# Step sizes first, second convolutions and GLU handed out between the SSD chunks

## The chip, the cores and the metric

The kernel runs on one core of a Trainium2 chip. The metric is the device time of one execution in microseconds; the median of three runs of the kernel before is 2591.2 us (2588.39 to 2594.27). TensorE (PE) multiplies, VectorE (DVE), ScalarE (ACT) and GpSimd (POOL) do the elementwise work, and SyncE (SP) starts most DMAs; ACT starts a few.

## The reference

One encoder layer for two sequences (256 and 1024 tokens, kept here as 1280 columns of one [1024, 1280] matrix), all in float32:

```
h = rmsnorm(x);  u, z, xbc, dt, gates = split(h @ w_in)
s5 = s5_mixer(u)            # bidirectional complex scan, gelu, then h * sigmoid(h @ w_glu + b)
s5 = s5 @ w_s5_out
xbc = silu(conv4(xbc));  dt = softplus(dt + bias)
y  = d_skip * xs + ssd(xs, dt, a, B, C) + reversed ssd      # chunks of 128 tokens
m2 = group_rmsnorm(y * silu(z)) @ w_m2_out
x  = x + (gate0 * s5 + gate1 * m2) @ w_o
x  = x + relu(rmsnorm(x) @ w_up)^2 @ w_down;   out = rmsnorm(x)
```

## The kernel before

Each large product is made of three float32r matmuls (`mm3`: low x high, high x low, high x high parts); `load_w` loads a weight block on SP, ACT makes its high part (L117) and POOL its low part (L118). A "tile" of the input projection is 128 output rows by 1280 tokens: 3 pieces of 512, 512 and 256 columns, 8 x 3 matmuls each, 72 in all, into the two PSUM banks called `mm`. The code is written in the order of the program; a list scheduler then fixes one order of instructions for every engine, by program order and by blocks marked urgent. Each engine follows its order strictly, so an instruction that waits holds back everything behind it, DMA issues on SP and on ACT included.

The stages, with the names that matter here:

- S5: `s5_setup`, `s5_run`, and beside it on PE the 16 gate tiles `G` (`gate_tile`).
- `conv_tile(j, q)`, the list `X(j)`: five projection tiles of group j, then convolution and silu on DVE and ACT in the buffers `xpad` (two) and `ac` (one), and stores to DRAM (`xbc_d`, `xz_d`). `z_tile(j, q)`, the list `Z(j)`: three tiles with silu. There are four groups j.
- `dt_proc`: one projection tile, then some 50 elementwise steps on DVE for dt, its running sums (`dte`, `dtf`) and their logarithms, stored as 24 rows to DRAM (`es_d`, `cs_d`, `ns_d`), and small matmuls (`dg`, `dtf`) for the chunk decays.
- 40 chunks (four groups of ten). `chunk_in` transposes a chunk (`xt`) and carries the backward state; `chunk_loads` loads `bc`, `ec`, `er`, `el`, `xz` for the present and next chunk; `chunk_out` makes the decay matrices (matmuls `ex`, exponential `e`), the matmuls `y`, the result `yt` and its sums of squares `ssg`; `norm_factors` makes the row factors of a group (`rows`, to `rs_d`). `er`, `el`, `eye` and `out_of` are constant tiles, filled once.
- Between chunks the list `left` hands out remaining `conv_tile` and `z_tile` calls, so many per chunk.
- GLU, for two halves of 640 tokens: six loads `y` from DRAM and their parts (`yx`), six gated tiles (`w_glu`, tanh `th`, `s5`, parts `sx`), eight output tiles (`w_s5`, DVE into `t1`, stored in `ma_d`). Each of the 14 tiles is 36 matmuls of 320 columns. They stand behind the chunks in program order; the scheduler lifts them into gaps.
- `normed`: for 432 tokens the factors `rg` (from `rs_d`) and twelve tiles `wt` (from `w_d`) become twelve pairs of parts `gx` (DVE, ACT, DVE). `merge` multiplies them by `w_m2` (36 matmuls per output tile, parts `mer`), `residual` by `w_o`; three times. Then the MLP, from about 1675 us to the end.

The lines that the prediction speaks of: dt on DVE L370 to L428; the stores of `parts` L408; the fills L550 to L557; the chunk matmuls L588 to L621; `yt` L624 to L627; the GLU L684 to L709; `normed` L655 to L662 with `hi_lo` L648 and L649; `hnw` L670.

Of the kernel before, what the change touches and what calls it, by code (L numbers as in the profile page):

```python
# [8 lines left out]
F32 = mybir.dt.float32  # L9
F32R = mybir.dt.float32r  # L10
# [45 lines left out]
def tile_encoder(ctx: ExitStack, tc: tile.TileContext, a: dict, dbg=None):  # L56
# [49 lines left out]
    def urgent():  # L106
        return tc.high_priority(offset=URG) if URG else ExitStack()
# [53 lines left out]
    with ExitStack() as pctx:  # L161
# [185 lines left out]
        def emit(l):  # L347
            for f, *r in l:
                f(*r)
        emit(G(0, 16) + X(0)[:2])  # L350
        kp = pctx.enter_context(tc.tile_pool(name="ssdk", bufs=1))
        dst, dec = (kp.tile([P, 10, 48], F32, name=n) for n in ("dst", "dec"))

        def dt_proc():

            with tc.tile_pool(name="dtp", bufs=1) as dp:
# [43 lines left out]
                def parts(src, dst_):  # L400
                    hl2 = [T(f"{src.name}p{i}", F32R) for i in range(2)]
                    act.activation(hl2[0], src, AF.Copy)
                    dve.tensor_tensor(hl2[1], src, hl2[0], SUB)
                    for i in range(2):
                        for h in range(2):
                            for d in range(2):
                                r = 64 * h + 32 * d
                                nc.sync.dma_start(dst_(i, d)[:, :, h * HT:h * HT + HT], hl2[i][r:r + 24].bitcast(F32))  # L408
# [4 lines left out]
                parts(e, lambda i, d: cs_d[:, d, i])  # L413
                dve.tensor_scalar(q, v, 1e-37, None, MAX)
                act.activation(q, q, AF.Ln)
                dve.tensor_tensor(q, q, e, SUB)
                parts(q, lambda i, d: ns_d[:, d, :, i])
                dve.tensor_tensor(f, f, n, SUB)
                act.activation(f, f, AF.Exp)
                dve.tensor_tensor(f, f, v, MUL)  # L420
# [117 lines left out]
            rsqrt(nc, r, ms, t)  # L538
            nc.sync.dma_start(rs_d[j, k0:k0 + n], r)

        NR = 2
        ers = [sp.tile([P, 6, P], F32R, name=f"er{i}", bufs=1) for i in range(NR)]
        els = [sp.tile([P, 2, P], F32R, name=f"el{i}", bufs=1) for i in range(NR)]
        for i in range(NR):
            B6 = [P, 6, P]
            pick = lambda o: ident[:, 4 + o:16 + o:2].unsqueeze(2).to_broadcast(B6)
            dve.tensor_tensor(ers[i], pick(0), pick(1), ADD)  # L550
            for d in range(2):
                dve.tensor_tensor(els[i][:, d], *(ident[:, c:c + 1].to_broadcast([P, P]) for c in (2 * d, 2 * d + 1)), ADD)

        eye = sp.tile([P, P], F32R, name="eye", bufs=1)
        dve.tensor_copy(eye, ident)
        out_of = sp.tile([P, 2, P], F32R, name="out_of", bufs=1)
        dve.tensor_scalar(out_of.rearrange("p i l -> p (i l)"), C("low", 0, 2 * P), BIG, BIG, MUL, SUB)  # L557
        nth = [0]

        def chunk_loads(j, k):  # L560
# [18 lines left out]
        def chunk_out(j, k, xt, sf, sb, ssum):  # L579
# [52 lines left out]
            dve.tensor_tensor(sq[:, 0], sq[:, 0], sq[:, 1], ADD)  # L632
            dve.tensor_tensor(ssum, sq[:, 0], sq[:, 2], ADD)

        ins = [(j, k) for j in range(4) for k in (1, 0, 9, 8, 7, 6, 5, 4, 3, 2)]
# [35 lines left out]
    with ExitStack() as gctx:  # L671
        gp = gctx.enter_context(tc.tile_pool(name="glu", bufs=1, side="right"))
        hb = gctx.enter_context(tc.tile_pool(name="glub", bufs=2, side="right"))
        hbg = gp.tile([P, 6], F32, name="hbg")
        dve.tensor_scalar(hbg, V("bglu", 0, 6), 0.5, None, MUL)
        for hf in range(2):
            t0 = hf * HT
            if hf:
                gx = normed(*cs[0])
            y0, yx, sx = [], [], []  # L680
            with urgent():
                for k in range(6):
                    r = gp.tile([P, HT], F32, name=f"y{k}")
                    nc.scalar.dma_start(r, y_d[k, hf].rearrange("p t n -> p (t n)"))  # L684
                    y0.append(r)
                    yx.append(split(gp, f"yx{k}", r, (pool, dve)[k % 2]))
            for m in range(6):
                w = load_tile(a["w_glu"][m])
                th = hb.tile([P, HT], F32, name="th5")
                s5 = hb.tile([P, 80, 8], F32, name="s5")  # L690
                for c0 in (0, 320):
                    pt = bank("mm")
                    mm3(pt[:, :320], w, yx, slice(c0, c0 + 320))
                    with urgent():
                        act.activation(th[:, c0:c0 + 320], pt[:, :320], AF.Tanh, scale=0.25, bias=hbg[:, m:m + 1])
                with urgent():
                    dve.scalar_tensor_tensor(s5.rearrange("p c t -> p t c"),
                                             th.rearrange("p (t c) -> p t c", t=8), 1.0,
                                             y0[m].rearrange("p (t c) -> p t c", t=8), ADD, MUL)
                    sx.append(split(gp, f"sx{m}", s5.rearrange("p c t -> p (c t)"), (pool, dve)[m % 2]))  # L700
            for m in range(8):
                w = load_tile(a["w_s5"][m])
                t1 = hb.tile([P, HT], F32, name="t1")
                nc.sync.dma_start(t1, gate_d[m, :, t0:t0 + HT])
                for c0 in (0, 320):
                    pt = bank("mm")
                    mm3(pt[:, :320], w, sx, slice(c0, c0 + 320))
                    dve.scalar_tensor_tensor(t1[:, c0:c0 + 320], t1[:, c0:c0 + 320], 1.0, pt[:, :320], ADD, MUL)
                nc.sync.dma_start(ma_d[m, :, t0:t0 + HT], t1)  # L709
# [624 lines left out]
```

## Time and profile before

| what | us |
|---|---|
| median of three runs | 2591.2 |
| the profiled execution | 2594.99 |
| its span, first to last instruction | 2593.2 |
| PE busy | 2490.3 |
| DVE busy | 1488.2 |
| ACT busy | 949.0 |
| POOL busy | 780.6 |

PE's busy time is the union of its matmuls, which overlap each other; a matmul's own duration is longer than the distance to the next. The granted clock is the share of full speed (2.4 GHz) that TensorE had; 0.5 is 1.2 GHz. A wait is put down to what ended it last.

### The profile page before, as it was taken

How to read it: one execution, taken by the hardware profiler on the slowest of the kernel's cores; microseconds unless marked ns; L12 is line 12 of the kernel's file. 1: busy time of each engine (PE TensorE's matmuls, PEld its weight loads, DVE VectorE, ACT ScalarE, POOL GpSimd, SP SyncE). 2: the span in 40 equal slices, each digit the busy share in tenths (PEclk: the TensorE clock that was granted, in tenths of full speed). 3: DMA queues.
4: the chain of work that ended last, by engine and by line, in shares of the span. 5: the costliest groups of instructions: out<-in, count | busy, mean ns of one | idle time of the engine just before them, and what ended most of it. 6: DMA issues, size and time to landing. Idle time of an engine off the chain costs nothing.

```text
span 2593.2 us, 37087 instructions
## 1 busy us (share of the span) xinstructions
PE 2490.3 (96%) x14119; PEld 2135.8 (82%) x14119; DVE 1488.2 (57%) x2445; ACT 949.0 (37%) x1867; POOL 780.6 (30%) x558
## 2 busy tenths in 40 slices
PE   8999999979999999988989999999999999999998
PEld 6788888868888888877879899988888888888887
DVE  7899999782457667678652654433333333323336
ACT  7655554343445445454332434311111111111114
POOL 2511112111111111134244757632222222222235
PEclk9999999989999999999999999999999999999999
DMA  4323333233345545465556766431111111111113
GB/s 148 105 84 99 96 96 94 91 121 106 132 138 168 156 134 164 144 188 153 180 160 190 223 188 206 151 122 37 37 37 41 37 37 37 41 37 37 37 45 114
DMA packets 254434, 286.21 MB, mean 110 GB/s; under 512 B 29864, under 2 KB 186704, under 8 KB 254256
## 3 DMA queue, kind: packets, MB, share of 16 engines
q1 hardware_dynamic: 252528, 279.90, 34.5%
q10 hardware_dynamic: 1728, 3.93, 0.5%
q8 instruction: 112, 1.84, 0.3%
q14 instruction: 66, 0.54, 0.1%
HBM read 210.26 MB, written 73.50 MB: 109 GB/s over the span
## 4 chain that ended last, share of the span: by engine, by line
PE 69%; DVE 17%; DMA 6%; ACT 3%; issue 2%; POOL 1%; SPq 1%; DVEq 0%; ACTq 0%; POOLq 0%
PE pa L142 24%; PE mm L133 20%; PE pa L133 9%; PE mm L142 8%; DVE z L1179 1%; PE ps L475 1%; PE y L621 1%; DVE z L1178 1%; DMA wt<-w_d 1%; DMA raw<-w_m 1%; PE ex L608 1%; PE ba L597 1%; PE ex L610 1%; DVE gx L649 1%; DVE wt L662 1%
## 5 line engine op out<-in xcount | busy, mean ns | idle before, releaser
L118 POOL TENSOR_TENSOR wl<-raw,wh 128x512 fp32r<-128x512 f32 (+1 forms) x422 | 582.0, 1384 | 1683.9 <-ACT wh L117 1600.9
L117 ACT ACTIVATE wh<-raw 128x512 fp32r<-128x512 f32 (+1 forms) x422 | 258.8, 615 | 922.8 <-PE pa L142 522.8
L133 PE MATMUL mm<-hh,wl 128*128 128x512 f32 (+1 forms) x1272 | 465.1, 366 | 14.9 <-ACT hh L220 7.5
L133 PE MATMUL mm<-hl,wh 128*128 128x512 f32 (+1 forms) x1272 | 465.9, 366 | 0.0
L133 PE MATMUL mm<-hh,wh 128*128 128x512 f32 (+1 forms) x1272 | 465.7, 366 | 0.0
L133 PEld LDWEIGHTS mm<-hh,wl 128*128 128x128 f32 x1272 | 242.5, 191 | 56.2 <-POOL wl L118 6.7
L133 PEld LDWEIGHTS mm<-hl,wh 128*128 128x128 f32 x1272 | 242.3, 190 | 41.5 <-issue 3.2
L133 PEld LDWEIGHTS mm<-hh,wh 128*128 128x128 f32 x1272 | 242.5, 191 | 40.9 <-issue 4.1
L142 PE MATMUL pa<-hid,wh 128*128 128x512 f32 (+1 forms) x1008 | 254.6, 357 | 0.0
L802 DVE TENSOR_TENSOR acc<-acc,pa 128x512 f32<-128x512 f32 (+1 forms) x252 | 138.2, 595 | 140.4 <-PE pa L142 140.4
L142 PEld LDWEIGHTS pa<-hid,wh 128*128 128x128 f32 x1008 | 170.3, 188 | 29.8
L786 DVE SCALAR_TENSOR_TENSOR r<-pa,rs 128x512 f32<-128x512 f32 (+1 forms) x72 | 39.6, 596 | 230.0 <-PE pa L142 230.0
L133 PE MATMUL pa<-gx,wh 128*128 128x432 f32 (+1 forms) x576 | 158.5, 356 | 0.0
L142 PE MATMUL pa<-xnh,wl 128*128 128x512 f32 (+1 forms) x576 | 155.9, 357 | 0.0
L142 PE MATMUL pa<-xnl,wh 128*128 128x512 f32 (+1 forms) x576 | 155.0, 357 | 0.0
L142 PE MATMUL pa<-xnh,wh 128*128 128x512 f32 (+1 forms) x576 | 154.0, 357 | 0.0
L142 PE MATMUL pa<-hid,wl 128*128 128x512 f32 (+1 forms) x504 | 143.4, 356 | 0.0
L318 DVE SCALAR_TENSOR_TENSOR ac<-xpad,hcw,ac 128x1282 f32<-128x1282 f32 x60 | 93.9, 1565 | 44.8 <-ACT ac L316 44.4
L142 PEld LDWEIGHTS pa<-xnh,wh 128*128 128x128 f32 x576 | 96.5, 188 | 17.9
L133 PEld LDWEIGHTS pa<-gx,wh 128*128 128x128 f32 x576 | 108.3, 188 | 3.6
L142 PEld LDWEIGHTS pa<-xnh,wl 128*128 128x128 f32 x576 | 96.5, 188 | 17.8
L142 PEld LDWEIGHTS pa<-xnl,wh 128*128 128x128 f32 x576 | 96.4, 188 | 17.9
(457 smaller groups left out, 4865.5 us busy)
## 6 DMA issues: line engine op xcount, KB each, us to landing
raw<-w_in SPq DMA_DIRECT2D x110, 256.0 KB
raw<-w_m SPq DMA_DIRECT2D x72, 256.0 KB
raw<-w_dn SPq DMA_DIRECT2D x72, 256.0 KB
raw<-w_up SPq DMA_DIRECT2D x64, 256.0 KB
ec<-es_d SPq DMA_DIRECT2D x80, 192.0 KB
xz<-xz_d SPq DMA_DIRECT2D x40, 384.0 KB
raw<-w_o SPq DMA_DIRECT2D x48, 256.0 KB
gate_d<-gv SPq DMA_DIRECT2D x16, 640.0 KB
```

What stands on the lines that cost most here:

```text
L117: act.activation(wh[:, :n], raw[:, :n], AF.Copy)
L118: pool.tensor_tensor(wl[:, :n], raw[:, :n], wh[:, :n], SUB)
L133: pe.matmul(out, l, r[:, sl], start=(n == 0), stop=(n == last))
L142: pe.matmul(o, l, r[:, sl], start=(n == 0), stop=(n == last))
L318: dve.scalar_tensor_tensor(ac[:, :n], xp[:, k:k + n], w(k), ac[:, :n], MUL, ADD)
L475: pe.matmul(st[:, :384], xt[:, 384:512], xs, start=True, stop=True)
L597: pe.matmul(bk[:, q * P:(q + 1) * P], st[:, q * P:(q + 1) * P], cf, start=True, stop=True)
L608: pe.matmul(ps[:, d].rearrange("p (h l) -> p h l", h=3), eye, out_of[:, d:d + 1].to_broadcast([P, 3, P]), start=True, stop=False)
L610: pe.matmul(ps[:, d], el[:, d], er[:, 3 * hh_:3 * hh_ + 3].rearrange("p h l -> p (h l)"), start=False, stop=True)
L621: pe.matmul(y[e0 * 64:e0 * 64 + 64, q * P:(q + 1) * P], xt[:, h * 64:h * 64 + 64], G[h // 3][:, h % 3], start=True, stop=True)
L786: dve.scalar_tensor_tensor(r[:, s], pt, 0.0, rs2[:, s], MAX, MUL)
L802: dve.tensor_tensor(ac[:, m, s], ac[:, m, s], pt, ADD)
```

## The change

Four moves, no arithmetic changed:

1. `dt_proc` comes right after the gate tiles, ahead of all convolution tiles (it stood behind the first two). The constant tiles `er`, `el`, `eye`, `out_of` are filled ahead of it, in a pool of their own, not in the memory that dt's temporaries leave. The stores of the second `parts` call (`ns_d`) are issued on ACT, not on SP.
2. Only `X(0)` and `Z(0)` come before the chunks; `X(1)` (five tiles) joins the list `left`, now 24 tiles.
3. `left` is handed out as two tiles after each of the first two chunks, one after the third, then 0.8 per chunk (0.7 before).
4. When `left` is empty (after the 27th chunk) the GLU memory is opened, and two of 30 GLU steps (per half: one load, six gated tiles, eight output tiles) follow each chunk. What is left of them comes after the last chunk, behind the first `normed`.

```diff
-        emit(G(0, 16) + X(0)[:2])
+        emit(G(0, 16))
         kp = pctx.enter_context(tc.tile_pool(name="ssdk", bufs=1))
+        ers = [kp.tile([P, 6, P], F32R, name=f"er{i}", bufs=1) for i in range(NR)]
...
-                parts(q, lambda i, d: ns_d[:, d, :, i])
+                parts(q, lambda i, d: ns_d[:, d, :, i], nc.scalar)
...
         dt_proc()
-        emit(X(0)[2:] + Z(0) + X(1))
-        left = Z(1) + X(2) + Z(2) + X(3) + Z(3)
+        emit(X(0) + Z(0))
+        left = X(1) + Z(1) + X(2) + Z(2) + X(3) + Z(3)
...
-        ers = [sp.tile([P, 6, P], F32R, name=f"er{i}", bufs=1) for i in range(NR)]
...
+        gctx, glu = ExitStack(), []
+        def glu_open():
+            rctx.close()
+            gp = gctx.enter_context(tc.tile_pool(name="glu", bufs=1, side="right"))
...
+            for hf in range(2):
+                glu.append(lambda hf=hf: load(hf))
+                for m in range(6):
+                    glu.append(lambda m=m: gated(m))
+                for m in range(8):
+                    glu.append(lambda m=m, hf=hf: s5_out(m, hf * HT))
...
                 chunk(j, k)
-                while left and 10 * (n_left - len(left)) < 7 * (10 * j + k + 1):
+                i = 10 * j + k + 1
+                while left and 10 * (n_left - len(left)) < min(20 * i, 50 + 8 * (i - 3)):
                     emit([left.pop(0)])
-        rctx.close()
+                    if not left:
+                        glu_open()
+                for _ in range(2):
+                    if not left:
+                        glu.pop(0)()
...
+    gx = normed(*cs[0])
+    for f in glu:
+        f()
+    gctx.close()
```

`load`, `gated` and `s5_out` hold the statements that the loop over the halves had.

How the order moves at the places that matter. On PE at the end of the last chunk, before: the last row-sum matmul (`ps<-ssg`) has S5 output matmuls (`sx`) on both sides, and 504 of the second half's follow.

```order
L133 MATMUL mm<-sx4h,wh 128x320
L133 MATMUL mm<-sx5h,wl 128x320
L133 MATMUL mm<-sx5l,wh 128x320
L133 MATMUL mm<-sx5h,wh 128x320
L534 MATMUL ps<-ssg,cst 6x128
L133 MATMUL mm<-sx0h,wl 128x320
L133 MATMUL mm<-sx0l,wh 128x320
L133 MATMUL mm<-sx0h,wh 128x320
```

The same place in the changed kernel: the first merge's matmuls on `gx` follow at once, two output tiles in turn.

```order
L133 MATMUL mm<-sx4h,wh 128x320
L133 MATMUL mm<-sx5h,wl 128x320
L133 MATMUL mm<-sx5l,wh 128x320
L133 MATMUL mm<-sx5h,wh 128x320
L553 MATMUL ps<-ssg,cst 6x128
L133 MATMUL pa<-gx,wl 128x432 x2
L133 MATMUL pa<-gx,wh 128x432 x2
L133 MATMUL pa<-gx,wl 128x432
L133 MATMUL pa<-gx,wh 128x432 x2
```

On SP at the same place, before: the factors' store and the loads of `normed` stand between weights of the second GLU half.

```order
L116 DMA raw<-w_glu 128x384
L539 DMA rs_d<-rows 6x128
L704 DMA t_12997<-gate_d 128x640
L655 DMA rg<-rs_d 128x4x432
L661 DMA wt<-w_d 128x432 x3
L116 DMA raw<-w_glu 128x384 x2
L661 DMA wt<-w_d 128x432 x2
```

And in the changed kernel: weights of the merge (`w_m`) and of the residual (`w_o`) stand ahead of `rg`, loads of the merge (`t`, `ma`) behind the first three `wt`.

```order
L116 DMA raw<-w_m 128x512 x2
L558 DMA rs_d<-rows 6x128
L116 DMA raw<-w_o 128x512 x4
L712 DMA rg<-rs_d 128x4x432
L718 DMA wt<-w_d 128x432 x3
L743 DMA t_13413<-gate_d 128x432
L744 DMA ma<-ma_d 128x432
L743 DMA t_13478<-gate_d 128x432
L744 DMA ma<-ma_d 128x432
```

On SP after dt, before: the stores of `ns_d` and `cs_d`, then a store of a convolution tile (`xbc_d<-xpad`).

```order
L408 DMA ns_d<-dtq_4969p_5138 4x6x640
L408 DMA cs_d<-dte_4966p_5124 4x6x640 x4
L408 DMA ns_d<-dtq_4969p_5138 4x6x640 x3
L408 DMA ns_d<-dtq_4969p_5139 4x6x640 x4
L569 DMA ec<-es_d 64x6x128
L322 DMA xbc_d<-xpad 128x256
L323 DMA xbc_d<-xpad 128x1024
```

In the changed kernel the eight `ns_d` stores are gone from SP to ACT, and the loads of `er`, `el` and `ec` for two chunks stand ahead of the convolution tile's store.

```order
L426 DMA cs_d<-dte_4766p_4924 4x6x640 x4
L572 DMA er_4748<-cs_d 4x6x128
L572 DMA er_4749<-cs_d 4x6x128
L573 DMA el_4750<-ns_d 12x2x128
L573 DMA el_4751<-ns_d 12x2x128
L571 DMA ec<-es_d 64x6x128 x3
L322 DMA xbc_d<-xpad 128x256
```

## Rows read from the trace of the kernel before

**Rows 1.** The page, first part: busy us, share of the span, instructions.

```profile
PE 2490.3 (96%) x14119; PEld 2135.8 (82%) x14119; DVE 1488.2 (57%) x2445; ACT 949.0 (37%) x1867; POOL 780.6 (30%) x558
```

**Rows 2.** Windows: length, engines' busy us (count), granted clock, DMA share, GB/s.

```profile
535.00:576.00 41.00, 24.46 (x110) 20.05 (x109) 33.10 (x36) 17.38 (x34) 5.95 (x3) 0.75 0.32 99
...
700.00:1100.00 400.00, 400.00 (x2299) 326.55 (x2298) 262.57 (x488) 200.43 (x423) 66.35 (x56) 1.00 0.49 150
1100.00:1116.00 16.00, 8.78 (x52) 8.06 (x52) 4.46 (x7) 7.56 (x19) 6.43 (x5) 0.79 0.89 265
1116.00:1275.00 159.00, 143.22 (x948) 123.79 (x946) 124.98 (x227) 74.70 (x161) 52.68 (x42) 0.97 0.54 162
1275.00:1337.00 62.00, 50.58 (x317) 47.58 (x315) 43.09 (x58) 24.56 (x49) 26.20 (x20) 0.97 0.55 167
1337.00:1376.00 39.00, 38.74 (x253) 38.77 (x254) 6.86 (x15) 7.65 (x14) 14.31 (x14) 0.96 0.61 187
```

**Rows 3.** PE's waits, 1100 to 1340 us: total us, times, longest.

```profile
PE mm L133 <- ACT th L695: 9.5, 7, 2.7
PE ex L608 <- ACT e L613: 8.0, 5, 2.9
PE mm L133 <- ACT yx0h L154: 6.5, 1, 6.5
```

**Rows 4.** DVE in order of time around dt: start us, us, instruction, idle before.

```profile
471.40 0.48 DVE L1208 SCALAR_TENSOR_TENSOR yg<-gsq,pa 128x320 f32<-128x320 f32 x1
...
476.72 0.15 DVE L946 TENSOR_SCALAR an<-vec 128x1 f32<-128x1 f32 x1 [1.77 <-DMA y_d<-yg]
...
480.88 0.16 DVE L955 SCALAR_TENSOR_TENSOR an<-an,ai 128x1 f32<-128x1 f32 x1
...
497.41 1.52 DVE L370 SCALAR_TENSOR_TENSOR dte<-dtv 128x640 f32<-128x640 f32 x1 [2.45 <-ACT dtv L367]
...
562.86 0.96 DVE L550 TENSOR_TENSOR er<-cst 128x768 fp32r<-128x768 f32 x1 [1.86 <-DMA ns_d<-dtq_4969p]
...
565.55 0.29 DVE L557 TENSOR_SCALAR out_of<-cst 128x256 fp32r<-128x256 f32 x1
```

**Rows 5.** The chain of waits behind dt: start us, us, what.

```profile
552.98 0.29 SPq L408
...
558.40 0.58 SPq L408
559.03 3.56 DMA ns_d<-dtq_4969p
...
563.53 3.03 DMA xbc_d<-xpad
566.58 3.58 DMA xf<-xbc_d
...
571.32 5.07 PE mm L133 x24
```

**Rows 6.** The chain of waits: a convolution tile, S5 outputs, a merge's matmuls.

```profile
607.79 14.08 PE mm L133 x72
...
1337.26 38.75 PE mm L133 x252
...
1471.08 60.24 PE pa L133 x306
```

**Rows 7.** DVE in order of time after the last chunk's matmuls.

```profile
1274.87 0.56 DVE L624 TENSOR_TENSOR yt<-y,xz 128x384 f32<-128x384 f32 x1 [1.71 <-PE y L621]
...
1289.81 0.70 DVE L670 TENSOR_SCALAR hnw<-vec 128x12 f32<-128x12 f32 x1 [2.53 <-DMA rs_d<-rows]
...
1298.35 1.83 DVE L662 SCALAR_TENSOR_TENSOR wt<-wt,hnw,rg 128x432 f32<-128x432 f32 x3 [6.16 <-DMA wt<-w_d]
...
1325.36 0.67 DVE L649 TENSOR_TENSOR gx<-wt,gx 128x432 fp32r<-128x432 f32 x1
```

**Rows 8.** DVE in order of time: first and last of the second merge's nine tiles.

```profile
1437.77 0.66 DVE L662 SCALAR_TENSOR_TENSOR wt<-wt,hnw,rg 128x432 f32<-128x432 f32 x1
...
1457.59 1.52 DVE L649 TENSOR_TENSOR gx<-wt,gx 128x432 fp32r<-128x432 f32 x1
```

**Rows 9.** ACT in order of time: one DMA issue on ACT's queue.

```profile
1104.98 0.44 ACTq L684 DMA_DIRECT2D y<-y_d  x1
```

More of the change, by code (lines that the diff above doesn't have):

```diff
@@ L349, in emit @@
                 f(*r)
-        emit(G(0, 16) + X(0)[:2])
+        emit(G(0, 16))
         kp = pctx.enter_context(tc.tile_pool(name="ssdk", bufs=1))
         dst, dec = (kp.tile([P, 10, 48], F32, name=n) for n in ("dst", "dec"))
+        NR = 2
+        ers = [kp.tile([P, 6, P], F32R, name=f"er{i}", bufs=1) for i in range(NR)]
+        els = [kp.tile([P, 2, P], F32R, name=f"el{i}", bufs=1) for i in range(NR)]
+        for i in range(NR):
+            B6 = [P, 6, P]
+            pick = lambda o: ident[:, 4 + o:16 + o:2].unsqueeze(2).to_broadcast(B6)
+            dve.tensor_tensor(ers[i], pick(0), pick(1), ADD)
+            for d in range(2):
+                dve.tensor_tensor(els[i][:, d], *(ident[:, c:c + 1].to_broadcast([P, P]) for c in (2 * d, 2 * d + 1)), ADD)
+        eye = kp.tile([P, P], F32R, name="eye", bufs=1)
+        dve.tensor_copy(eye, ident)
+        out_of = kp.tile([P, 2, P], F32R, name="out_of", bufs=1)
+        dve.tensor_scalar(out_of.rearrange("p i l -> p (i l)"), C("low", 0, 2 * P), BIG, BIG, MUL, SUB)
         def dt_proc():
@@ L398, in dt_proc, with parts @@
                             dve.tensor_tensor_scan(o[s], mk[s], n[s], 0.0, MUL, ADD)
-                def parts(src, dst_):
+                def parts(src, dst_, q_):
                     hl2 = [T(f"{src.name}p{i}", F32R) for i in range(2)]
@@ L407, in parts @@
                                 r = 64 * h + 32 * d
-                                nc.sync.dma_start(dst_(i, d)[:, :, h * HT:h * HT + HT], hl2[i][r:r + 24].bitcast(F32))
+                                q_.dma_start(dst_(i, d)[:, :, h * HT:h * HT + HT], hl2[i][r:r + 24].bitcast(F32))
                 for h in range(2):
@@ L412, in dt_proc @@
                         nc.sync.dma_start(es_d[:, d, :, h * HT:h * HT + HT], e[r:r + 24])
-                parts(e, lambda i, d: cs_d[:, d, i])
+                parts(e, lambda i, d: cs_d[:, d, i], nc.sync)
                 dve.tensor_scalar(q, v, 1e-37, None, MAX)
@@ L539, in norm_factors @@
             nc.sync.dma_start(rs_d[j, k0:k0 + n], r)
-        NR = 2
-        ers = [sp.tile([P, 6, P], F32R, name=f"er{i}", bufs=1) for i in range(NR)]
[L546 to L557, printed above, removed]
         nth = [0]
@@ L633, in chunk_out, with load, gated, s5_out @@
             dve.tensor_tensor(ssum, sq[:, 0], sq[:, 2], ADD)
+        gctx, glu = ExitStack(), []
+        def glu_open():
+            rctx.close()
+            gp = gctx.enter_context(tc.tile_pool(name="glu", bufs=1, side="right"))
+            hb = gctx.enter_context(tc.tile_pool(name="glub", bufs=2, side="right"))
+            hbg = gp.tile([P, 6], F32, name="hbg")
+            dve.tensor_scalar(hbg, V("bglu", 0, 6), 0.5, None, MUL)
+            y0, yx, sx = {}, {}, {}
+            def load(hf):
+                with urgent():
+                    for k in range(6):
+                        r = y0[k] = gp.tile([P, HT], F32, name=f"y{k}")
+                        nc.scalar.dma_start(r, y_d[k, hf].rearrange("p t n -> p (t n)"))
+                        yx[k] = split(gp, f"yx{k}", r, (pool, dve)[k % 2])
+            def gated(m):
+                w = load_tile(a["w_glu"][m])
+                th = hb.tile([P, HT], F32, name="th5")
+                s5 = hb.tile([P, 80, 8], F32, name="s5")
+                for c0 in (0, 320):
+                    pt = bank("mm")
+                    mm3(pt[:, :320], w, [yx[k] for k in range(6)], slice(c0, c0 + 320))
+                    with urgent():
+                        act.activation(th[:, c0:c0 + 320], pt[:, :320], AF.Tanh, scale=0.25, bias=hbg[:, m:m + 1])
+                with urgent():
+                    dve.scalar_tensor_tensor(s5.rearrange("p c t -> p t c"),
+                                             th.rearrange("p (t c) -> p t c", t=8), 1.0,
+                                             y0[m].rearrange("p (t c) -> p t c", t=8), ADD, MUL)
+                    sx[m] = split(gp, f"sx{m}", s5.rearrange("p c t -> p (c t)"), (pool, dve)[m % 2])
+            def s5_out(m, t0):
+                w = load_tile(a["w_s5"][m])
+                t1 = hb.tile([P, HT], F32, name="t1")
+                nc.sync.dma_start(t1, gate_d[m, :, t0:t0 + HT])
+                for c0 in (0, 320):
+                    pt = bank("mm")
+                    mm3(pt[:, :320], w, [sx[k] for k in range(6)], slice(c0, c0 + 320))
+                    dve.scalar_tensor_tensor(t1[:, c0:c0 + 320], t1[:, c0:c0 + 320], 1.0, pt[:, :320], ADD, MUL)
+                nc.sync.dma_start(ma_d[m, :, t0:t0 + HT], t1)
+            for hf in range(2):
[4 more added lines that the diff above has]
+                    glu.append(lambda m=m, hf=hf: s5_out(m, hf * HT))
@@ L670, in tile_encoder @@
     dve.tensor_scalar(hnw, V("m2nw", 0, 12), 0.5, None, MUL)
[L671 to L709, printed above, removed]
+    gx = normed(*cs[0])
+    for f in glu:
+        f()
+    gctx.close()
     xp = ctx.enter_context(tc.tile_pool(name="xn", bufs=1, side="right"))
```

## Prediction

> **What bounds the kernel now.** I read the page first: TensorE (PE) is busy for 96% of the span [rows 1], so everything that can be won is the rest, about 103 us, and what a low clock costs beside it. Then the windows by stage [rows 2]: where convolution tiles lie between chunks (700 to 1100 us) PE is busy for all 400 us at full clock. Two stretches are not like that. From 535 to 576 us, while the step sizes dt are worked out, PE is busy for 24.5 of 41 us, at a mean clock of 0.75. From 1100 to 1376 us, the last thirteen chunks and the GLU with the S5 output, it is idle for 7.2 + 15.8 + 11.4 + 0.3 = 34.7 us. The change touches these two and leaves the MLP alone. Then PE's waits in the second stretch [rows 3]: many short ones, on ACT's exponentials and tanh, and one of 6.5 us for the first GLU input. The chain of waits for the first stretch [rows 5] and DVE's order of time for what follows the last chunk [rows 7] come last.
>
> The profiled execution took 2595.0 us (span 2593.2), the median of the runs is 2591.2; I sum changes and take them from the median.
>
> **GLU between the last chunks: the gain.** No matmul is added or removed. In the kernel before, the order on PE has 61 + 504 = 565 matmuls of 320 columns (the end of the first half's S5 output, and the whole second half) behind the last chunk's `y`; in the changed order 22 are left there. At 38.75 us for 252 of them [rows 6], 0.154 us each, 543 matmuls or 83 us go in front of the last chunk's end, as filler. Does it fill? Until the last `y`, which ends at 1274.8 [rows 7], PE idles 15.8 us after 1116, and after it, while the second half's GLU runs alone, 11.4 us [rows 2]. Two steps per chunk are 72 matmuls or 11 us, much as the convolution filler in the stage that shows no idle at all. So of 27.2 us idle I let 5 stay (a GLU block has only two PSUM banks, and waits for tanh [rows 3] also between chunks) and take 22. The clock: 0.97, 0.97 and 0.96 over 159, 62 and 39 us are 4.8 + 1.9 + 1.6 = 8.3 us of lost full clock; with the gaps gone I take back 7. Sum 29 us. Bounds: 10 (the order of the changed kernel meets transfers that are later than it assumes) and 35 (everything). The 7.2 us at 1100 to 1116 stay: the first GLU input is still loaded when the last convolution tile gives up its memory.
>
> **What lay under the GLU: the new wait.** The normalized SSD output `gx` for the first merge can only be made when the last chunk's row factors are in DRAM. In the kernel before that was hidden: `y` ends at 1274.8, the first DVE operation that needs the factors (`hnw`) runs at 1289.8, the first `wt` is scaled at 1298.4, the twelfth `gx` low part is done at 1326.0 [rows 7], and PE had matmuls of the second GLU half until 1376. In the changed order PE goes from the last 22 S5 matmuls and the row-sum matmul straight to `gx`. Step by step from the last `y`: to `hnw` 15.0 us before, with S5 operations between; I take 11. From there to the first `wt` 8.5, kept, since the four `w_o` loads now stand before `rg` on SP, where six `w_glu` loads shared the engines before. Then twelve tiles: 27.7 us in the first merge, 2.3 us a tile; the second merge's last nine, with no GLU beside them, took 1437.8 to 1459.1, 2.4 us a tile [rows 8]. I take 25. Sum 44.5 us after the last `y`. In that time PE has its 22 S5 matmuls (3.4 us) and, because the changed order takes two output tiles side by side and the start of a third, 36 + 36 + 16 = 88 `gx` matmuls at 60.24/306 = 0.197 us [rows 6], 17.3 us. So 44.5 - 20.7 = 24 us are idle, and coming back at half clock, as after the idle stretch at 535 to 576 us, costs 2: 26 us lost. Bounds: 14 (DVE alone sets the pace, 12 x (0.61 + 0.67) = 15 us [rows 7], no clock loss) and 33 (all of the 51.2 us of before, and clock).
>
> **Step sizes before the convolutions.** On PE the dt tile moves ahead of two convolution tiles, 2 x 14.08 = 28.2 us [rows 6]. It then needs a PSUM bank that ACT frees only behind the last gelu of S5, and the DVE chain needs DVE, where S5's last operation ends at 471.9 [rows 4], perhaps 3 us sooner without the convolution operations between. In front of the chain now stand the `er`, `el`, `eye`, `out_of` fills (562.86 to 565.84, 3.0 us) and the exponential of `alog` (476.7 to 481.0, less one convolution operation of 1.5: 2.8). So the chain starts at about 475 instead of 497.4 [rows 4]: 22.4 us sooner against 28.2 us of work that PE has not had: 5.8 us lost. Behind the chain PE again waits with the same two tiles ahead of it, for the same reason: the third convolution buffer is free only when an earlier one is stored. On the kernel before that store stood behind ten issues on SP of 0.58 us and a landing of 3.56 us, until 563.5, and PE was dense again at 571.3 [rows 5]. Now the `ns_d` stores go out on ACT, eight at about 0.44 us [rows 9] = 3.5 instead of 5.8 us, and the fills no longer wait for memory of the dt stage; but the `el` and `ec` loads stand on SP ahead of the store and wait for the same landing. I give it 2 us. Behind the waiting ACT issues stand the exponential for `dst` and the convolution's tanh, which PE's `ex` and bank wait for, so no more. Sum: 4 us lost. Bounds: 4 won (the chain starts at once) and 10 lost (the store and the next `xf` load each 3 us later [rows 5]).
>
> The rows show that handing out DMAs takes time of its own here: 5.8 us of issues against 3.6 us of landing [rows 5]. The Trainium skill, "DMA: Bandwidth & Descriptors", section "Issuing engines are not separate DMA queues", says that starting DMAs from several engines saves only the sequencer's time to start them, "which is usually small relative to the DMA itself". By that rule moving the `ns_d` stores to ACT would be worth nothing, and the forecast 2 us later; the trace disagrees with "small" for these 12-row stores.
>
> **Second convolutions between chunks.** Five tiles move from in front of the chunks to between the first three, and the rate is 0.8 instead of 0.7. On PE the order has reached the 27th chunk with the same work done in both kernels, and the stage was dense with fewer fillers [rows 2]. Zero; what hides it is PE's own work. If the chunk inputs come just too late there, each of three tiles' stores and loads (3.0 + 3.6 us [rows 5]) could show: 0 to 10 us lost.
>
> **Sum.** 29 - 26 - 4 + 0 = -1, a microsecond lost and far inside the bounds: no change that can be measured. I say 2591, the median of before, within 2583 to 2599.
>
> **Rivals.**
> *The filling wins.* The tail fills fully (35), `gx` comes through at 1.3 to 1.7 us a tile because nothing else is on DVE (seam 18), dt breaks even: 17 us, 2574. For it: PE never idles in the convolution stage, and DVE was shared with the GLU in the first merge's rows. Against: the second merge's tiles were no faster without a GLU.
> *The new wait wins (slower).* The place is PE between the last S5 output and the first merge. The `gx` chain keeps all its 51 us, so 33 are lost there, and dt costs 6: 29 - 39 = 10 slower, 2601; with a tail that keeps half its gaps (gain 20), 2610. It decides when the wait between the last S5 matmul and dense `gx` matmuls exceeds what the tail saves, about 29 us. For it: the rows of before show exactly that length; against: they were made beside a GLU.
> *The change doesn't fill.* The scheduler already put GLU matmuls into the last chunks before (the first half ran there), and the gaps come from chains of DMA and ACT that more filler only shifts: gain 10, 2611. Against: with convolution filler the same chains cost nothing.
>
> **How the numbers follow.** A measurement of this kernel can tell about 0.2%, 5 us. Forecast 40% (2583 to 2599), filling wins 30%, new wait 22%, no filling 8%. Of the forecast's 40%, about 10 lie over 5 us faster, 24 within, 6 slower. Faster: 30 + 10 = 40%; same 24%; slower 22 + 8 + 6 = 36%. The range for 8 in 10 cuts a tenth off either side: 2568 to 2612.
>
> **What the profile of the changed kernel would show.** PE busy over 95% from the 27th chunk's start to the last `y`, which comes near 1340 us instead of 1275; then a hole of 20 to 30 us before PE is dense on `gx`, ended by DVE's `wt` and `gx` and the `wt` DMAs, and a lower granted clock around it. About 28 us earlier than before, the dt hole again with 15 to 20 us idle. I am wrong if the hole before the first merge is under 12 us, if PE idles over 15 us in the tail after its first GLU input, or if the dt hole is gone.

## The result and the profile after

The changed kernel took 2612.4 us (median of 4 runs, 2610.8 to 2615.4) beside 2589.8 us (2586.6 to 2594.3) for the kernel before. The ratio is 1.0089, 95% interval 1.0076 to 1.0103: slower by 20 to 27 us. The forecast was 2591, no change that can be measured.

The profiled execution of the changed kernel took 2611.2 us (span 2609.4), that of the kernel before 2595.0. These two differ by 16 us, the medians by 22.6, since the profiled execution of before lies 5.2 us above the median of its runs and that of after 1.2 below. Place and cause are read from the traces, which show the 16 us; sizes are taken from the ratios of the runs.

The first part of the page (busy us, share of the span, instructions) answers to [rows 1]:

```profile
PE 2491.0 (95%) x14119; PEld 2134.5 (82%) x14119; DVE 1499.8 (57%) x2445; ACT 947.1 (36%) x1867; POOL 778.1 (30%) x558
```

TensorE's busy time is the same to 0.7 us, so nearly all of the change is idle time. To place it I read from PE's rows in order of time when certain matmuls start (us from the span's start):

| start of | before | changed | later by |
|---|---|---|---|
| the last S5 matmul | 464.3 | 464.2 | -0.1 |
| the first GLU matmul (`yx0`) | 1110.6 | 1121.3 | 10.8 |
| the last chunk's last `y` | 1274.6 | 1361.5 | (other work in front) |
| the first merge's first matmul (`gx`) | 1375.8 | 1383.8 | 8.0 |
| the matmul behind the first merge (`mer`) | 1435.3 | 1452.9 | 17.6 |
| the MLP's first matmul (`xn`) | 1674.7 | 1690.8 | 16.1 |

So 10.8 us are lost between S5 and the GLU, 2.8 won between the first GLU matmul and the first merge's, 9.6 lost inside the first merge, 1.5 won behind it.

The windows of the changed kernel answer to [rows 2] (length, busy us and count of PE, PEld, DVE, ACT, POOL, granted clock, DMA share, GB/s). The first is the step-size stage, the others from 1121 us on are cut at the table's times:

```profile
450.00:600.00 150.00, 124.69 (x595) 103.62 (x595) 104.67 (x130) 52.95 (x90) 26.12 (x16) 0.91 0.30 99
...
700.00:1100.00 400.00, 400.00 (x2287) 326.87 (x2286) 252.51 (x462) 193.76 (x402) 65.19 (x57) 1.00 0.48 149
1121.30:1361.50 240.20, 228.75 (x1508) 208.97 (x1508) 161.48 (x256) 105.01 (x223) 98.03 (x78) 0.97 0.55 166
1361.50:1383.80 22.30, 4.25 (x28) 3.35 (x25) 9.10 (x22) 2.33 (x5) 2.54 (x2) 0.63 0.61 209
1383.80:1452.70 68.90, 61.32 (x287) 54.51 (x288) 38.75 (x48) 24.55 (x44) 29.73 (x22) 0.97 0.55 173
```

The same stretches of the kernel before, cut at its own times:

```profile
450.00:600.00 150.00, 133.46 (x661) 111.70 (x660) 104.31 (x135) 56.85 (x102) 29.26 (x18) 0.93 0.34 109
...
1110.60:1274.60 164.00, 147.50 (x963) 127.97 (x963) 127.71 (x229) 79.80 (x173) 58.08 (x45) 0.95 0.55 165
1274.60:1375.80 101.20, 89.52 (x573) 86.25 (x570) 50.09 (x72) 32.21 (x62) 40.32 (x34) 0.97 0.58 176
1375.80:1435.10 59.30, 57.57 (x289) 53.72 (x288) 23.02 (x24) 19.39 (x34) 31.04 (x24) 1.00 0.57 183
```

In the step-size stage PE idles 25.3 us instead of 16.5, 8.8 more. The clock is counted, as in the forecast, as 1 minus the granted share, times busy time, which is an estimate: it cost 11.2 us there instead of 9.3. Together that is about 11, the table's 10.8.

From the first GLU matmul to the first merge PE idled 16.5 + 11.7 = 28.2 us before. In the changed kernel it idles 11.5 us up to the last `y`: 16.7 won. The clock cost 7.4 + 2.7 = 10.1 us before and costs 6.9 now: 3.2 won. That is the worth of the filling in these two traces, 20 us. About half of the 6.9 lies in the first 7.0 us, where the granted clock is 0.50 behind the wait for the first GLU input. At the seam, where the GLU ends and the first merge begins, come 22.3 us with 4.3 us of work (18.0 idle, and 1.6 for the clock of 0.63), and a merge with 7.6 us idle instead of 1.7 and a clock of 0.97 (5.9 + 1.8): 27 us lost. The difference, 7, is what the table has.

PE's waits in the step-size stage, 455 to 600 us (engine and line waiting, releaser, total us, times, longest):

```profile
PE mm L133 <- ACT dtv L385: 9.7, 1, 9.7
PE pa L460 <- DVE dtf L438: 6.4, 1, 6.4
PE mm L133 <- ACT xpad L310: 2.6, 1, 2.6
PE pa L452 <- DVE dg L446: 2.4, 1, 2.4
```

The longest was not in the forecast: PE stands at the third column piece of dt, with two PSUM banks full, until ACT has taken the first piece into `dtv`. Why ACT comes so late shows on DVE in order of time (answers to [rows 4]; start us, us, instruction, idle before and what ended it):

```profile
468.06 0.49 DVE L1231 SCALAR_TENSOR_TENSOR yg<-gsq,pa 128x320 f32<-128x320 f32 x1 [0.53 <-ACT gsq L1230]
473.57 0.96 DVE L363 TENSOR_TENSOR er<-cst 128x768 fp32r<-128x768 f32 x1 [5.03 <-DMA y_d<-yg]
...
476.47 0.15 DVE L969 TENSOR_SCALAR an<-vec 128x1 f32<-128x1 f32 x1
...
480.38 0.82 DVE L388 SCALAR_TENSOR_TENSOR dte<-dtv 128x640 f32<-128x640 f32 x1
```

S5's last operation ends at 468.6, as the forecast had it. Then DVE (and ACT, 5.5 us) wait for the last `y_d` store. The operation that waits on DVE, `er`, reads only constants, so it is its memory that it waits for: the tiles of this stage lie in S5's memory, which is free only when its last store has landed. The chain starts at 480.4, 17.0 us sooner than before and not 22.4, against 28.2 us of PE work that no longer stands in front: 11.2 us short. Two paths end there together: DVE's fills and `alog`, and PE's third piece, whose part of `dtv` ACT has written at 480.3.

The chain of waits at its other end answers to [rows 5] (start us, us, what):

```profile
532.21 1.18 ACTq L426
...
534.70 5.34 DMA ns_d<-dtq_4769p
540.05 0.60 ACTq L426
...
540.68 1.28 ACT L437
541.98 0.74 ACT dtf L437
542.74 0.83 DVE dtf L438
543.62 1.34 PE pa L460 x5
...
547.66 3.94 DMA xbc_d<-xpad
...
552.42 16.90 PE mm L133 x72
```

ACT hands out the eight `ns_d` stores from 532.2 to 540.7, and its exponential for `dst`, PE's transposes of it (the 6.4 us) and the rest stand behind. Of the 8.4 us, 5.9 are the issues themselves. The chain puts the last issue, at 540.05, down to the landing of the fourth store, issued at 534.70. The semaphores in the trace say why: this program gives its DMAs on ACT four completion semaphores in turn, so that the sixth, seventh and eighth store wait until the second, third and fourth have landed, 1.7 us in all. On SP it gives eight, and no store waits there. From the chain's start to dense convolution matmuls it took 552.4 - 480.4 = 72.0 us, before 571.3 - 497.4 = 73.9. That leaves 11.2 - 1.9 = 9.3 us; the other 1.5 of the 10.8 come up between there and the first GLU matmul.

At the seam DVE's order answers to [rows 7]; SP's shows which loads stand in front of `rg` and `wt`:

```profile
1361.78 0.56 DVE L626 TENSOR_TENSOR yt<-y,xz 128x384 f32<-128x384 f32 x1 [2.15 <-PE y L623]
...
1372.74 0.17 DVE L727 TENSOR_SCALAR hnw<-vec 128x12 f32<-128x12 f32 x1 [1.35 <-DMA rs_d<-rows]
1382.31 1.83 DVE L719 SCALAR_TENSOR_TENSOR wt<-wt,hnw,rg 128x432 f32<-128x432 f32 x3 [9.40 <-DMA wt<-w_d]
1384.06 1.64 DVE L706 TENSOR_TENSOR gx<-wt,gx 128x432 fp32r<-128x432 f32 x3
```

```profile
1372.77 1.76 SPq L116 DMA_DIRECT2D raw<-w_o  x4
1374.57 0.43 SPq L712 DMA_DIRECT2D rg<-rs_d  x1
1375.05 1.55 SPq L718 DMA_DIRECT2D wt<-w_d  x3
```

From the last `y` to `hnw` 11.0 us, to the first `wt` another 9.6; the forecast had 11 and 8.5. `hnw` reads only a constant (`vec`) and the four loads of `raw<-w_o` only weights, and yet both start just when the last `rs_d<-rows` store has landed: so they wait for memory and not for data. The twelve `gx` are done 22.9 us after the first `wt` (25 forecast). PE's waits from 1340 to 1455 us:

```profile
PE pa L133 <- DMA t<-gate_d: 15.8, 1, 15.8
PE pa L133 <- ACT gx L705: 3.2, 2, 1.7
PE pa L133 <- POOL wl L118: 2.9, 5, 1.0
```

The first is the hole. It is put down to a gate load, which the waiting matmul doesn't read and which the trace has land at 1383.82, when the matmul has begun (1383.80); ACT ends the first `gx` at 1383.70. In the kernel of the first experiment below, with the same seam, the hole is put down to ACT's `gx` (16.9 us).

### The profile page after: what moved, and what is told of

Its sections match the earlier page's. It is cut to its first block, busy times and chain, and to the rows that moved or that the text cites. A ratio compares the mean times of both kernels' runs of the same rounds, so it can differ in the third digit from the quotient of the medians.

```text
span 2609.4 us, 37053 instructions
## 1 busy us (share of the span) xinstructions
PE 2491.0 (95%) x14119; PEld 2134.5 (82%) x14119; DVE 1499.8 (57%) x2445; ACT 947.1 (36%) x1867; POOL 778.1 (30%) x558
## 4 chain that ended last, share of the span: by engine, by line
PE 69%; DVE 18%; DMA 6%; ACT 3%; issue 2%; SPq 1%; POOL 1%; ACTq 0%; DVEq 0%; POOLq 0%
PE pa L142 24%; PE mm L133 19%; PE pa L133 9%; PE mm L142 8%; DVE z L1202 2%; PE y L623 1%; DVE z L1201 1%; DMA wt<-w_d 1%; PE ps L494 1%; DMA ec<-es_d 1%; PE ex L610 1%; PE ex L612 1%; PE ba L599 1%; DVE gx L706 1%; DVE tm L1099 1%
## 5 line engine op out<-in xcount | busy, mean ns | idle before, releaser
L118 POOL TENSOR_TENSOR wl<-raw,wh 128x512 fp32r<-128x512 f32 (+1 forms) x422 | 582.0, 1382 | 1690.8 <-ACT wh L117 1608.3
L133 PE MATMUL mm<-hh,wh 128*128 128x512 f32 (+1 forms) x1272 | 464.3, 365 | 0.0
L133 PE MATMUL pa<-gx,wl 128*128 128x432 f32 (+1 forms) x288 | 103.4, 363 | 22.1 <-DMA t<-gate_d 15.8
```

Source lines behind the costliest of these rows:

```text
L118: pool.tensor_tensor(wl[:, :n], raw[:, :n], wh[:, :n], SUB)
L133: pe.matmul(out, l, r[:, sl], start=(n == 0), stop=(n == last))
```

## The experiments

Each kernel is compared by its ratio to runs of the kernel before taken beside it, since the experiments ran on different chips; "+23" means 23 us over before, what the ratio has above 1, times 2592. The changed kernel stands at +23 (20 to 27).

**The step sizes back behind two convolution tiles.**

```
-        emit(G(0, 16))
+        emit(G(0, 16) + X(0)[:2])
-        emit(X(0) + Z(0))
+        emit(X(0)[2:] + Z(0))
```

> The changed kernel, with the step sizes dt back behind two convolution tiles; all else as changed (fills ahead of dt, the ns_d stores on ACT, the GLU between chunks). Theory, from the trace after: moving dt cost 11 to 12 us, not the 4 of the forecast, because PE stood 9.7 us at the third bank of dt, which ACT could not empty until the last y_d store of S5 had landed (dt's buffers lie in S5's memory), and two convolution tiles used to cover that. Then this runs 9 to 13 us faster than the changed kernel (2600 to 2603), and the 9.7 us wait is gone. Rival 1: the dt term was 4 as forecast and the loss lies in the tail: 2607 to 2610. Rival 2: the 6.4 us wait behind ACT's eight ns_d issues is the larger part of the loss and stays here: 2605 to 2608.

2607.9 us (2602.5 to 2608.3), ratio 1.0054 (1.0041 to 1.0066): +14, so 9 us back, the lower end of the theory; by the two intervals it could also be 4 or 14. The place is plain in the trace: the first GLU matmul starts at 1109.8, 0.8 us earlier than before where the changed kernel is 10.8 later. PE's waits, 455 to 600 us, have no `dtv` any more:

```profile
PE pa L452 <- DVE dg L446: 6.0, 1, 6.0
PE pa L460 <- DVE dtf L438: 5.6, 1, 5.6
```

The wait behind ACT's issues stays, 5.6 us, while all of the 10.8 us at the first GLU matmul are back, so it was not what made the move dear (rival 2 falls by the trace; the runs alone don't exclude it).

**GLU steps kept for behind the last chunk.**

```
-                for _ in range(2):
-                    if not left:
-                        glu.pop(0)()
+                while not left and len(glu) > 8 + (30 - 8) * (40 - i) // 15:
+                    glu.pop(0)()
```

> The changed kernel, with the GLU's 30 steps spread so that 8 are left for behind the last chunk: 280 matmuls of 320 columns stand there instead of 22, about 40 us of work. Theory: the loss at the seam (PE idle some 21 us and a lower clock behind it, 26 us against before) comes from the chain from the last row factors over rg and wt to gx, which nothing covers; with cover PE is dense from the last y to the merge, and the time falls by 18 to 26 us against the changed kernel, less what the thinner filling gives back in the tail (0 to 8): 2587 to 2602. Rival: the filler is worth as much between the chunks as behind them, so that what the seam wins the tail loses: within 5 us of 2612.

In the changed kernel all thirty steps are handed out by the 40th chunk: by the code, `left` is empty after the 26th chunk, not the 27th, and two steps follow each of fifteen chunks.

2608.7 us, ratio 1.0064 (1.0051 to 1.0076): +17, only 6 back. The theory fell; the rival, within 5, is near. The windows of this kernel, from the first GLU matmul to the last `y`, to the first `gx` matmul, to the end of the merge:

```profile
1121.20:1329.90 208.70, 191.42 (x1249) 171.41 (x1250) 147.67 (x241) 96.86 (x208) 82.70 (x64) 0.96 0.53 157
1329.90:1381.40 51.50, 45.21 (x287) 44.11 (x285) 28.97 (x57) 14.83 (x28) 17.09 (x15) 0.93 0.71 220
1381.40:1447.10 65.70, 59.45 (x288) 52.95 (x288) 21.13 (x28) 20.23 (x35) 32.33 (x24) 1.00 0.59 190
```

The hole behind the last `y` shrinks from 18.0 to 6.3 us, but in front of it PE idles 17.3 us where it idled 11.5, and the merge still idles 6.2 (now 5.9 of it in waits for POOL's weight parts `wl`). The same matmuls can fill one place or the other.

**The `ns_d` stores back on SP.**

```
-                parts(q, lambda i, d: ns_d[:, d, :, i], nc.scalar)
+                parts(q, lambda i, d: ns_d[:, d, :, i], nc.sync)
```

> The changed kernel, with the eight ns_d stores issued on SP again, nothing else. Theory: on ACT they take 8.5 us in which the exponential for dst waits, and PE's transposes of dst behind it wait 6.4 us; on SP that wait falls, but the convolution store behind them on SP comes later: 0 to 5 us faster than the changed kernel (2607 to 2612). Rival, the forecast's step: the move to ACT gave 2 us back by handing the stores out sooner: 2 us slower (2614). Third, from the rule that the issuing engine does not matter: the same within 2 us.

2611.1 us, ratio 1.0076 (1.0062 to 1.0090): 3 us back, and the intervals overlap, so the runs don't tell it from nothing. The trace has the mechanism. ACT, DVE and PE's longest wait there:

```profile
534.24 0.74 ACT L437 ACTIVATE dtf<-dtf 128x640 f32<-128x640 f32 x1
```

```profile
536.79 0.82 DVE L438 TENSOR_TENSOR dtf<-dtf,dtv 128x640 f32<-128x640 f32 x1
```

```profile
PE ex L610 <- ACT dst L462: 4.4, 1, 4.4
```

The factor that PE transposes is ready at 537.6 instead of 543.6, and PE's wait for it is gone; but PE now waits 4.4 us instead of 0.6 for ACT's copy `dst` one step later, which stands behind a convolution step on ACT. The first GLU matmul comes 4.5 us earlier; at the MLP's first matmul 0.6 of that are left. The forecast's step, 2 us won by the stores on ACT, has the wrong sign here if any.

**Only the GLU handed out**, on the kernel before (`dt`, fills, stores and second convolutions as before; the changed kernel's `glu_open` and this):

```
+                for _ in range(2):
+                    if not left:
+                        glu.pop(0)()
```

> The kernel before, with the GLU and the S5 output handed out between the last chunks and nothing else of the change. Theory, from the two traces: the tail wins 17 to 24 us, the seam and the second merge lose 26 to 30: 2 to 12 us slower than before (2592 to 2602). Rival 1: the whole loss of the change lies here: 2608 to 2613. Rival 2: the seam was priced too high: faster than before, 2580 to 2588.

2601.2 us (2596.7 to 2603.9), ratio 1.0034 (1.0022 to 1.0046): +9 (6 to 12), the theory's range. Its trace has the hole again, 18.8 us behind the last `y`, and a merge of 68.4 us. So of the change's +23 about 9 belong to the GLU and, if the parts add up, about 14 to the rest.

**dt's banks.** The dt projection in the pool of six PSUM banks:

```
-                project(22, ev)
+                project(22, ev, "pa")
```

> The changed kernel, with the dt projection's three column pieces in the pool of six PSUM banks instead of the two-bank pool it shares with the convolutions. Theory: moving dt forward costs what PE waits at dt's third piece (9.7 us, until ACT has taken the first piece, which it may only after S5's last y_d store has landed, since dt's buffers lie in S5's memory). With six banks PE goes on to the convolution tile, and that wait falls: 7 to 11 us faster than the changed kernel, about where the kernel with dt back in its old place was (14 us above before): 13 to 17 us above before. Rival 1: ACT stands in order behind dt's evacuation, so the convolution's banks aren't emptied either and the same wait only moves by a few us: within 3 us of the changed kernel (20 to 24 above before). Rival 2: the loss of the move is the waits behind ACT's store issues, not this one: the same.

2609.5 us, ratio 1.0067 (1.0054 to 1.0079): +17, so 6 back (1 to 10 by the two intervals), just under the theory's 7 to 11 and over the rival's 3; the runs don't decide between them. In the trace 8.4 of the 10.8 us at the first GLU matmul are back. PE's waits say where the rest went:

```profile
PE pa L452 <- DVE dg L446: 6.0, 1, 6.0
PE pa L460 <- DVE dtf L438: 5.5, 1, 5.5
PE mm L133 <- ACT xpad L310: 2.9, 1, 2.9
```

The 9.7 us are gone, and the chain on DVE even starts 2.1 us sooner (478.3). But it now runs beside more of the convolution's operations (16.8 us of them instead of 9.3), reaches `dg` 7.2 us later, and PE's wait for `dg` grows from 2.4 to 6.0. That wait is 5.7 to 6.0 with one or two tiles in front of dt as well, so it isn't what sets this kernel apart from those. The bank was about half of the cost by the runs and more by the trace; what the rest is isn't shown.

**The first merge's `gx` made early**, on the kernel with only the GLU handed out. The first 432 columns need the row factors of chunks 0 to 3 of each group, and the last of these is the 34th of 40 chunks, so the data of `gx` is there early. Its tiles take over the memory of `y`, `yx`, `th5` and `s5` once the last gated step is done (two further tiles beside them). The pools of `normed` and `xn` open behind the first merge, and `mer` changes its side of the memory, to make room:

```
+            def gx_tile(m):
+                j = m // 3
+                if m % 3 == 0:
+                    rg0[0] = gp.tile([P, MC], F32, name="rg0")
...
+                hi, lo = (p_.tile([P, HT], F32R, name=f"g{m}", tag=t_)[:, :MC] for p_, t_ in slots[2 * m:2 * m + 2])
...
+                dve.scalar_tensor_tensor(wt, wt, hn[:, m:m + 1], rg0[0], MUL, MUL)
+                act.activation(hi, wt, AF.Copy)
+                dve.tensor_tensor(lo, wt, hi, SUB)
...
+                    if hf:
+                        glu.append(lambda m=m: [gx_tile(g) for g in range(12 * m // 8, 12 * (m + 1) // 8)])
...
-    gx = normed(*cs[0])
+    gx = gx0
```

> The kernel before with only the GLU handed out between the chunks (9 us above before), and the first merge's 24 gx tiles made between the chunks 37 to 40, in the memory of GLU tiles that the last gated step has freed (the first 432 columns need the row factors of chunks 0 to 3 of each group only, the last of which is the 34th chunk). Theory: the loss at the seam is a wait for memory and for DMAs, not for data; with gx made early PE goes from the last S5 matmuls straight into a dense merge, which gives back the 18 us of idle time before the first gx and 6 of the 9 us in the merge: 20 to 28 us faster than with the GLU alone, 10 to 20 us faster than before (2572 to 2582). Then its distance to before is the worth of the filling by itself: forecast 29, by the trace after 20. Rival: the merge waits next for its own weights and gate loads, which now start late, and the gx work slows the last chunks: no more than 8 us faster than the GLU alone (2592 to 2600).

2575.6 us (2572.7 to 2579.7), ratio 0.9936 (0.9922 to 0.9949): 17 us faster than before (13 to 20) and 25 faster than with the GLU alone. The windows run from the first GLU matmul to the last `y`, to the first merge matmul, to the merge's end; below them stands what PE waits for from 1340 to 1420:

```profile
1113.70:1345.60 231.90, 220.14 (x1461) 199.83 (x1462) 164.72 (x271) 106.58 (x222) 97.24 (x74) 0.99 0.61 178
1345.60:1353.00 7.40, 6.98 (x48) 6.33 (x45) 4.30 (x9) 2.43 (x5) 4.18 (x3) 1.00 0.44 142
1353.00:1413.90 60.90, 57.83 (x289) 53.48 (x290) 23.77 (x32) 17.49 (x30) 29.94 (x24) 1.00 0.57 178
```

```profile
PE pa L133 <- POOL wl L118: 3.2, 4, 1.6
```

The hole is gone and the merge takes 60.9 us (59.3 in the kernel before). That shows that the seam's loss was the `gx` chain, and that the chain needs nothing of the last six chunks. That memory set its place is shown by the waits of `hnw` and `raw<-w_o` above; this experiment moved the chain in the program and in memory at once. With the seam closed the gain left, 17 us, is about what the filling is worth by itself (by this trace's own windows 12.2 us idle and some 2 of clock stand against 28.2 and 10.1: 24 us, but this profiled execution lies 1.8 us below its median and that of before 5.2 us above).

**dt behind one convolution tile.**

```
-        emit(G(0, 16))
+        emit(G(0, 16) + X(0)[:1])
-        emit(X(0) + Z(0))
+        emit(X(0)[1:] + Z(0))
```

> The changed kernel, with dt behind one convolution tile (14 us of PE's work) instead of none or two. Theory: one tile covers the 9.7 us wait for dt's third bank, and the DVE chain behind starts as early as S5's end allows: as good as with two tiles or a little better, 8 to 14 us faster than the changed kernel (9 to 15 above before). Rival: what costs is that two tiles instead of four then stand beside the dt chain's end, and one tile gives half of it back: 3 to 6 us faster (17 to 20 above before).

2604.0 us, ratio 1.0042 (1.0030 to 1.0055): +11, 12 us back, as the theory said: one tile of 14 us covers the wait (no `dtv` wait is left in the trace), and a second adds nothing that can be told (the intervals of one and two overlap).

**dt back and the stores on SP** (the edits of the first and third experiment together).

> The changed kernel with dt behind two convolution tiles and the ns_d stores on SP, so that of the first half of the change only the fills ahead of dt and the second convolutions between the chunks are left; beside it stands the kernel with only the GLU changed (9 us above before). With dt back but the stores on ACT it was 14 us above. Theory: those 5 us are ACT's store issues, behind which PE's transposes of dst wait 5.6 us, and the second convolutions between the chunks cost nothing, as forecast: 8 to 11 us above before. Rival: the second convolutions (or the fills) cost the 5 us: 13 to 16 us above before.

2603.8 us, ratio 1.0051 (1.0038 to 1.0065): +13, the rival's number. The stores' place is not what lies between this kernel and the one with only the GLU changed (+9), whose interval this one's overlaps. In the traces this kernel is 1.0 us ahead of that one at the first GLU matmul and level behind the first merge (1441.0 against 1440.8); 2.6 us come up only in later merges, which none of the edits touches. Whether there is a loss at all stays open; the fills ahead of dt were not tried alone.

**Early `gx` and the best step-size stage**: the sixth kernel's edits on the changed kernel, with dt behind one tile and the stores on SP.

> The early gx tiles together with the best of the step-size stage: dt behind one convolution tile, the fills ahead of dt, the ns_d stores on SP, second convolutions and GLU between the chunks as changed. The early gx alone, over the old step-size stage, was 16 us faster than before. Theory: the step-size stage in this form is level with the old one or up to 4 us better, and the parts add up: 15 to 21 us faster than before (2571 to 2577). Rival: the step-size stage stays 2 to 4 us worse than the old one, as the traces with the stores on ACT have it: 12 to 14 us faster than before.

2572.8 us (2572.3 to 2573.9), ratio 0.9930 (0.9917 to 0.9942): 18 us faster than before, the fastest of all, though not to be told from the early `gx` alone. The theory's sum holds, and the rival's 12 to 14 lies outside the interval (15 to 22).

**Only the second convolutions between the chunks**, on the kernel before:

```
-        emit(X(0)[2:] + Z(0) + X(1))
+        emit(X(0)[2:] + Z(0))
-        left = Z(1) + X(2) + Z(2) + X(3) + Z(3)
+        left = X(1) + Z(1) + X(2) + Z(2) + X(3) + Z(3)
-                while left and 10 * (n_left - len(left)) < 7 * (10 * j + k + 1):
+                while left and 10 * (n_left - len(left)) < min(20 * (10 * j + k + 1), 50 + 8 * (10 * j + k - 2)):
```

> The kernel before, with only the second convolutions moved from in front of the chunks to between the first of them, at the changed kernel's rate. Theory, the forecast's step: nothing, since PE's own work hides it and the stage is dense: within 3 us of before (ratio 0.999 to 1.001). Rival, from the 4 to 5 us that lie between the kernel with only the GLU changed and the one with dt back and the stores on SP: 3 to 6 us slower than before.

2587.9 us, ratio 0.9991 (0.9982 to 1.0000): no loss, if anything 2 us won. The rival's 3 to 6 us slower is out.

## Why the prediction was wrong, step by step

The sum was 29 - 26 - 4 + 0. It came out, in the traces, as 20 - 27 - 11 + 0, with 2 won behind the first merge: 16 us slower there, 23 by the runs. Two terms were wrong, the start of the step sizes (by 7) and the filling (by 9).

**The step that failed first** is "So the chain starts at about 475 instead of 497.4". It started at 480.4. The forecast counted S5's last operation, the fills and the exponential of `alog`, but not the landing of the last `y_d` store, 5.0 us in which DVE did nothing. The row was there: in the kernel before `an` already waits 1.77 us for `y_d` [rows 4], the tail of the same wait, the rest of which lay under convolution operations. The forecast also saw that PE needs a bank "that ACT frees only behind the last gelu of S5", and missed that ACT may not write `dtv` before that landing either: 9.7 us. So 11.2 us were lost at the chain's start where the sum had 5.8, and the granted clock behind the wait, 0.50 from 469.5 to 479.8, was in no term. The two experiments with tiles in front (9 and 12 us back) show the size of the move's price; the six banks (6 back by the runs, 8.4 by the trace) show that PE's wait for the bank was half of it or more.

**The 2 us at the chain's end** came out as a number (72.0 us instead of 73.9) by luck, not by the mechanism. Eight issues were priced at 0.44 us [rows 9], 3.5 in all; they held ACT for 8.4 us, with 0.7 us for the second half of their data and 1.7 for the landing of earlier ones among them, and PE stood 6.4 us behind the exponential. The forecast saw that the exponential stands behind these issues, and took from it only that no more than 2 us are won, not that anything is lost. Back on SP the stores gained 3 us, not to be told from nothing. The forecast's "12-row stores" have 24 rows each, and its comparison sets ten issues (5.8 us) against one landing (3.6); a single issue of 0.58 us is short beside that landing. The Trainium skill's rule ("DMA: Bandwidth & Descriptors", "Issuing engines are not separate DMA queues"), by which the move was worth nothing, was nearer to the runs than the forecast. What neither priced is the work that stands behind an issue on a computing engine.

**The filling** is the term that was mis-sized within its bounds: 29 forecast, 20 by the windows of the changed kernel, 17 by the runs of the kernel with the seam closed. "So of 27.2 us idle I let 5 stay": 11.5 stayed. PE's waits from 1110 to 1340 us in the changed kernel name them:

```profile
PE mm L133 <- ACT yx0h L154: 5.3, 1, 5.3
PE ex L610 <- ACT e L615: 4.3, 2, 3.9
PE y L623 <- DVE e L618: 3.6, 3, 1.7
PE mm L133 <- ACT th L663: 2.0, 3, 1.2
```

The first of these lies in front of the stretch, as the forecast had it. The others are mostly the chunk's own chain: waits for its exponentials and products still cost 7.9 us. What makes these late, with filler enough in PE's order, wasn't tried. And "I take back 7" of the clock was 3: it stands at 0.97 over the 240 us, in part because the half clock behind the first GLU input lasts longer than before (7.0 us instead of some 5).

**The seam** was right in size and in its steps: 26 forecast, 27 measured, of it 24 us of idle time in both (18.0 + 5.9 measured), with the steps to `hnw`, to the first `wt` and through the twelve `gx` within 2.1 us. Its cause was wrong. The forecast said that `gx` "can only be made when the last chunk's row factors are in DRAM"; the early `gx` shows that the first merge needs none of the last six chunks. The chain waited for the memory of the chunks.

**The second convolutions** at zero were right (2 us won, 0 to 5 by the interval).

Of the rivals, "the new wait wins, slower" named the right place and outcome with the wrong split: its seam of 33 was 27, its dt of 6 was 11; that its 2610 for a gain of 20 lies so close to the measured time is luck, since the two errors cancel. "The filling wins" needed 35, 18 and 0 where the traces have 20, 27 and 11. "The change doesn't fill" has a time close to the measured one too, 2611, by a gain of 10 that was 20. Of the signs foretold, PE's busy share up to the last `y` was 95.2%, at the line; the last `y` came at 1361, not near 1340; the hole was 18 us and 6 more inside the merge; and the idle time of the step-size stage was 25 us (9.7 + 6.4 + 2.6 + 2.4 and smaller ones), over the 15 to 20 foretold. None of the three signs of being wrong came (18 us of hole, 11.5 of idle tail, a dt hole that is still there): they asked whether the terms exist, and the terms failed in size.

## What to carry to other kernels

Before moving a stage forward, ask what its buffers lie in: a stage that starts in the memory of the one before waits for that one's last store to land, and the row that shows it may be a short wait, since other work covers the rest. Work taken from behind a boundary to fill gaps in front of it uncovers what it hid there, so price both places; here they came out within 7 us of each other. Where such a chain is uncovered, look at which data it really needs: if only its memory is late, make it early in buffers that have just died.

## What was not expected of the hardware

The eight `ns_d` stores took 0.59 to 1.18 us each to hand out on ACT (median 0.60) and 0.58 to 0.61 on SP. The forecast's price of 0.44 came from one `y` load on ACT [rows 9]; the twelve of the kernel before took 0.33 to 0.72 (median 0.33). So the same store costs about the same to issue on ACT and on SP; the two kinds of transfer on ACT differ more (0.60 against 0.33). That the row of eight held ACT for 8.4 us, where the twelve stores on SP followed each other every 0.64 us, comes from the waits between the issues.
